# Sums of samples' halves and gate logits by a transposition and a VectorE sum in place of 0/1 products, and small gate and sample products merged or padded to 128 rows

## The chip, the cores and the metric

The kernel runs on one core of one Trainium2 chip. The metric is the time of one execution on the device in microseconds (us), the median of several runs. The names used here for the engines are those of the profile: PE is TensorE with its matrix products (PEld is the loading of its stationary operand), DVE is VectorE, ACT is ScalarE, POOL is GpSimd, and SP issues transfers.

## What is computed

The reference is one step of a hybrid decoder layer in float32: 1024 rows of a prompt and 32 rows of samples (8 sequences of 4 tokens) go through adaLN, one wide projection, an mLSTM branch with 4 heads, a sliding-window attention branch with 8 heads on 2 key/value heads, per-channel gates, and an output projection. Cut to what the change touches:

```
h, gate = adaln_in(x, c, w_ada, b_ada, g_norm)        # c: silu(c) @ w_ada, in three parts
(mq, mk, mv, mi, mf, mo, mz, aq, ak, av, az, gm, ga) = split_in(h @ w_in)
ig = mi + b_i                                         # the gate logits: 4 heads each
lf = log_sigmoid(mf + b_f)
b = cumsum(lf) per chunk of 128 rows                  # samples: per sequence of 4
...                                                   # mLSTM with exp(b - b + ig)
o = sink_attend(q, k, v)                              # samples: 128 cached rows and 4 own
u = sigmoid(gm) * (y_m @ w_mo) + sigmoid(ga) * (y_a @ w_ao)
x = x + gate * (u @ w_o)
```

## The kernel before, in words

PE is given its work in program order. The helper `mm` (line 275) issues one product and `tr` (line 280) one transposition, which is also a pass through PE; both advance a planning clock, `side.now`. A float32 product takes two passes on PE (`smpo` with 22 products has 44 rows in the profile), a transposition one. The large products, which make up most of the stream, are the projections of the prompt (`g_ak`, `g_av`, `g_aq`, `g_mq` ... and the pairs' `bx`, `by`, `bz`, `bw`); they use the full 128x128 array on pieces of 384, 288 or 512 columns. Between them stand small products of other work: attention units (`sc`, `pt`, `oT`), the mLSTM heads (`tk`, `tv`, `S`, `U`, `n`, `sU`, `sn`, `stk`), the samples, and the gates. Where these stand is set by `Side`, a planner: each kind of side work is a generator, which yields a lag and the PSUM banks that it needs next, and is resumed between large products when the planner's clock has passed the lag and the bank is free. PSUM has four tags of two banks each; the side work uses tags "b" (`pb`) and "o" (`po`). DVE and ACT carry out their instructions in the order of their queue, and a new tile in a bank waits until all readers of the tile before it in that bank are done.

The places that the change touches:

- **Gate logits.** `gate_piece` (line 596) multiplies the normalised rows with the gate columns in products of 32 columns each (`gg`), four partial sums in the four quarters of the partitions; ACT copies them to SBUF (`zg0`, `zg1`, `zg2`). `gate_sums` (line 607) then adds the four quarters: per block of 128 rows one product of `zg` with a 0/1 matrix of 8 columns into the PSUM tile `gp`; four blocks after the first piece, four after the second, one of 32 rows (the samples) after the third. `gates` (line 612) starts with that third call and goes on in DVE and ACT to `ig` and `lf`, then takes cumulative sums by products with triangular 0/1 matrices (`bp`, `gtp`), and later transposes a result (`fp`). Its pieces `bp`, `gtp`, `rp`, `bq`, `fp` and `fq2` stand between large products.
- **`kv_turn`** (line 797) transposes the values of the attention, first tile `vtp0`; it is started beside `gates`.
- **Samples' halves.** The projections of the 32 samples are not part of the large products: `Pair.samples` (16 products of a shape that uses 32 columns of the array, `smp`, or 8 for the output pairs, `smpa`) leaves four partial results in the four quarters of the partitions, that is two halves for each of two weight matrices; ACT copies them to `smps`. `samples_end` (lines 1392 and 1675) adds the halves with one product with a 0/1 matrix of 64 columns into the PSUM tile `smpo`, and the pair's own code reads that. There are 22 such calls: 4 pairs `head_in`, 8 `gate`, 2 `query_gate`, 4 `head_gate` and 4 output pairs.
- **Samples' attention** (line 915): `pts` are transpositions of the probabilities, `os` the products with the values, per half four with the cache (128 rows) and four with the samples' own values `vns` (32 rows).
- **`ada_gate`** (line 1943): twice `ada_products` (line 363), 8 products (4, a yield, 4) into one bank, `ada_ga`, 512 columns, on a quarter of the array's columns each.

Of the kernel before, what the change touches and what calls it, by code (L numbers as in the profile page):

```python
# [10 lines left out]
F32 = mybir.dt.float32  # L11
# [4 lines left out]
ALU = mybir.AluOpType  # L16
AX = mybir.AxisListType
# [18 lines left out]

C_ID, C_S9, C_TRI, C_CM, C_AM, C_TS, C_CS, C_RS, C_S32, C_BM, C_S64 = 0, 128, 137, 265, 393, 649, 681, 713, 745, 777, 785
C_END = 849
# [135 lines left out]
def body(tc, a):  # L174
    nc = tc.nc
    with ExitStack() as ctx:
# [429 lines left out]

        def gate_sums(gp, zg, cs):
            for c in cs:
                n = 128 if c < 8 else NS
                mm(gp[:n, c], zg[c // 4][:, c % 4 * 128:c % 4 * 128 + n], cst[:, C_S9:C_S9 + 8], start=True, stop=True)  # L610

        def gates(gp, zg, bias):
            gate_sums(gp, zg, (8,))
            ig = cp.tile([128, 36], F32, name="ig")
            gt2 = ht([128, 512], "gt2")
            x, e, r, q = (gt2[:, 256 + 36 * i:292 + 36 * i] for i in range(4))
            for t, o in ((ig, 0), (x, 4)):
# [6 lines left out]
            S.activation(e, e, AF.Exp, scale=-1.0)  # L624
            lf = sm([128, 36], "lf", 1)
            V.tensor_scalar(r, e, 2.0, None, op0=ALU.add)
# [12 lines left out]
            mm(bp[:, 0:36], tri, lf, start=True, stop=True)  # L639
            mm(bp[:NS, 64:68], cst[:NS, C_TS:C_TS + NS], lf[:NS, 32:36], start=True, stop=True)  # L640
            an = cp.tile([128, 36], F32, name="an")
            V.tensor_tensor(an, ig, bp[:, 0:36], op=ALU.subtract)
            V.tensor_tensor(an[:NS, 32:36], ig[:NS, 32:36], bp[:NS, 64:68], op=ALU.subtract)
            yield 4.0, "b"

            tp = pb([128, 4, 128], "gtp")
            tr(tp[:32, 0], an[:, 0:32], ident)
            mm(tp[:32, 1], lf[:, 0:32], tri, start=True, stop=True)
            tr(tp[:4, 2, 0:NS], an[:NS, 32:36], ident[:NS, :NS])
            mm(tp[:4, 3, 0:NS], lf[:NS, 32:36], cst[:NS, C_TS:C_TS + NS], start=True, stop=True)  # L650
            gt4 = ht([32, 4, 128], "gt4")
            aT, bT, zero, cm = (gt4[:, i] for i in range(4))
            nm, wi = gt2[:32, 0:128], gt2[:32, 128:256]
# [3 lines left out]
            V.tensor_copy(bT, tp[:32, 1])  # L657
            V.tensor_copy(aTs, tp[:4, 2, 0:NS])
            V.tensor_copy(bTs, tp[:4, 3, 0:NS])
            G.memset(zero, 0.0)  # L660
# [48 lines left out]
            fp = pb([128, 128], "fp")  # L709
            tr(fp[:, 0:32], bT, ident[:32, :32])  # L710
            fl = cp.tile([128, 32], F32, name="fl")
# [41 lines left out]
        def attention_begin():  # L753
            at["rope"] = [rope_load(p) for p in range(3)]
            at["vT"] = []
            at["sink"] = cp.tile([128, 2, 4], F32, name="sink")
            dma(at["sink"], a["sinks"].to_broadcast((128, 8)).rearrange("p (k g) -> p k g", g=4))
            at["qpad"] = cp.tile([128, NB, 2, 4, NT], F32, name="qpad")
            G.memset(at["qpad"], 0.0)
            at["kTs"] = cp.tile([128, NS], F32, name="kTs")  # L760
            at["vns"] = cp.tile([NS, 128], F32, name="vns")

# [34 lines left out]
        def kv_turn():  # L797
            kl, kTs, vT, kns, vns = at.pop("kl"), at["kTs"], at.pop("vT"), ht([128, 128], "kns")[:NS], at["vns"]
            for p, n in enumerate((3, 3, 2)):
                tp = pb([128, 3, 128], f"vtp{p}")  # L800
                for j in range(n):
                    tr(tp[:, j], vT[p][:, j * 128:(j + 1) * 128], ident)
                vn = ht([128, 3, 128], f"avn{p}")
                S.copy(vn[:, :n], tp[:, :n])
                dma(vnD[:, 3 * p:3 * p + n], vn[:, :n])
                if p < 2:
                    yield 4.0, "b"
            dma(a["v_p"], vn[:, 1])
            tp = pb([128, 3, 128], "kvtp")
            tr(tp[:, 0], kl[:, 128:256], ident)  # L810
            tr(tp[:NS, 1], kTs, ident)
            tr(tp[:NS, 2], vT[2][:, 256:288], ident)
            kn = ht([128, 128], "kl")
            V.tensor_copy(kn, tp[:, 0])
            V.tensor_copy(kns, tp[:NS, 1])
            V.tensor_copy(vns, tp[:NS, 2])
            dma(a["k_p"], kn)
            dma(a["k_s"][0:124], a["cache_k"][4:128])
            dma(a["v_s"][0:124], a["cache_v"][4:128])
            dma(a["k_s"][124:128].rearrange("t b e -> b t e"), kns)  # L820
            dma(a["v_s"][124:128].rearrange("t b e -> b t e"), vns)

# [92 lines left out]
        def sample_attention():  # L915
# [42 lines left out]
            for u in range(2):  # L958
                tr(pt[:, u], p[:, u, 0:WIN], ident)
                tr(pt[:NS, 2 + u], p[:, u, WIN:], ident)  # L960
            pT = kc[0]
            S.copy(pT[:, 0:2], pt[:, 0:2])
            V.tensor_copy(pT[:NS, 2:4], pt[:NS, 2:4])
            yield 7.0, "o"
            o = po([128, 2, 128], "os")
            for u in range(2):
# [3 lines left out]
                for w in range(4):  # L970
                    r = slice(32 * w, 32 * w + 32)
                    mm(o[r, u], pT[:NS, 2 + u, r], vns, start=False, stop=True, share=4)
            S.copy(p[:, :, 0:128], o)
# [394 lines left out]
        OPERANDS = {1: "b11", 2: "b21", 3: "b22", 4: "t4", 5: "t1", 6: "t2", 7: "t3"}  # L1368

        class Pair:  # L1370
            def __init__(self, kind, i):
# [20 lines left out]
            def samples_end(self):  # L1392
                o = pb([128, 64], "smpo")
                mm(o, self.sums, cst[:, C_S64:C_S64 + 64], start=True, stop=True)
                self.kind.samples(self, o.rearrange("p (c s) -> p c s", c=2))

# [249 lines left out]
        class AttPair:  # L1646
# [28 lines left out]
            def samples_end(self):  # L1675
                o = pb([128, 64], "smpo")
                mm(o, self.sums, cst[:, C_S64:C_S64 + 64], start=True, stop=True)
                us = ut[self.i % 2][:, self.i // 2 * 2:self.i // 2 * 2 + 2, SEQ:T]
                V.scalar_tensor_tensor(us, self.ts, 1.0, o.rearrange("p (c s) -> p c s", c=2), op0=ALU.add, op1=ALU.mult)

# [195 lines left out]
        for q, kk in enumerate(two):  # L1876
# [42 lines left out]
            if more:  # L1919
                x_mul(1, kept[1], two[q + 1])  # L1920
            else:
                pair_end(1, acc[1])
                gp = pb([128, 9, 8], "gp")
                gate_sums(gp, zg, range(4))
                gate_piece(wg, zg, 1)
            pair(kk, 2, acc[2])
        pair_end(2, acc[2])
        gate_sums(gp, zg, range(4, 8))
        gate_piece(wg, zg, 2)
# [13 lines left out]
        def ada_gate():  # L1943
            for j in range(2):
# [9 lines left out]
                acc = pb([128, 512], f"ada_ga{j}")  # L1954
                yield from ada_products(raws, acc)
                for r in range(0, 128, 32):
# [423 lines left out]
```

## Time and profile before

| | |
|---|---|
| time, median of 3 runs | 822.45 us (822.27 to 822.85) |
| the profiled execution's own time | 822.86 us |
| its span in the profile | 821.1 us |
| granted TensorE clock in it | 0.997 |
| busy PE, PEld, DVE, ACT, POOL | 98%, 81%, 73%, 51%, 6% of the span |

The profile is of one execution. A row of the timeline has the start in us from the span's start, the duration in us, the engine, the line, the operation, the tiles as out<-in (buffer numbers left out), the shapes and a count of instructions that ran on end; in square brackets stands the idle time ahead of it, if any, and what ended it. For PE the shape is rows\*columns of the array that the stationary operand takes, then the operand that streams through. Durations of PE's rows overlap, since passes are pipelined: what one costs is read from the starts of its neighbours.

### The profile page before, as it was taken

How to read it: one execution, taken by the hardware profiler on the slowest of the kernel's cores; microseconds unless marked ns; L12 is line 12 of the kernel's file. 1: busy time of each engine (PE TensorE's matmuls, PEld its weight loads, DVE VectorE, ACT ScalarE, POOL GpSimd, SP SyncE). 2: the span in 40 equal slices, each digit the busy share in tenths (PEclk: the TensorE clock that was granted, in tenths of full speed). 3: DMA queues.
4: the chain of work that ended last, by engine and by line, in shares of the span. 5: the costliest groups of instructions: out<-in, count | busy, mean ns of one | idle time of the engine just before them, and what ended most of it. 6: DMA issues, size and time to landing. Idle time of an engine off the chain costs nothing.

```text
span 821.1 us, 15097 instructions
## 1 busy us (share of the span) xinstructions
PE 803.2 (98%) x5145; PEld 666.1 (81%) x5145; DVE 598.6 (73%) x1495; ACT 419.2 (51%) x1020; POOL 46.5 (6%) x111
## 2 busy tenths in 40 slices
PE   6999999999999999999999999999999999999996
PEld 3779898888788878888888878788887789997775
DVE  4899886756755557475657889898668997876666
ACT  4764355556565564546555545554446652224334
POOL 0120000000000000000001011010002101000000
PEclk9999999999999999999999999999999999999998
DMA  9994757547545415537764685864436789647622
GB/s 338 395 330 136 228 167 221 166 155 208 173 138 171 148 60 162 163 131 254 238 213 152 229 265 186 266 216 141 142 100 193 237 294 393 211 140 284 205 104 109
DMA packets 113474, 165.49 MB, mean 202 GB/s; under 512 B 21185, under 2 KB 55745, under 8 KB 113365
## 3 DMA queue, kind: packets, MB, share of 16 engines
q1 hardware_dynamic: 107748, 153.78, 57.0%
q10 hardware_dynamic: 4176, 6.56, 2.2%
q0 software_dynamic: 1472, 4.20, 1.3%
q8 instruction: 40, 0.66, 0.3%
q14 instruction: 38, 0.30, 0.1%
HBM read 115.51 MB, written 50.00 MB: 202 GB/s over the span
## 4 chain that ended last, share of the span: by engine, by line
PE 88%; DVE 5%; DMA 3%; issue 2%; ACT 1%; SPq 0%; DVEq 0%; ACTq 0%
PE by L275 12%; PE bx L275 11%; PE bw L275 11%; PE g_w_mo L275 6%; PE bz L275 5%; PE g_aq L275 3%; PE foW L275 3%; PE foX L275 2%; PE foY L275 2%; PE smp L275 2%; PE g_mq L275 2%; PE sc L275 2%; PE oT L275 2%; PE n L275 2%; PE pt L280 2%
## 5 line engine op out<-in xcount | busy, mean ns | idle before, releaser
L220 ACT ACTIVATE p<-p,nmx 128x256 f32<-128x256 f32 (+1 forms) x64 | 31.1, 486 | 17.8 <-DVE nmx L220 15.2
L220 DVE CUSTOM_DVE_ANT_0 p<-sc,cst,sink 128x256 f32<-128x256 f32 (+1 forms) x64 | 26.1, 462 | 9.2 <-PE sc L275 9.1
L275 PE MATMUL g_aq<-h_h,wh_aq 128*128 128x384 f32 (+1 forms) x96 | 32.3, 336 | 0.0
L275 PE MATMUL g_aq<-h_h,wl_aq 128*128 128x384 f32 (+1 forms) x96 | 30.9, 322 | 0.0
L275 PE MATMUL g_aq<-h_l,wh_aq 128*128 128x384 f32 (+1 forms) x96 | 30.8, 321 | 0.0
L275 PE MATMUL g_w_mo<-ym_l,wh_w_mo 128*128 128x384 f32 (+1 forms) x96 | 30.8, 321 | 0.0
L275 PE MATMUL g_w_mo<-ym_h,wh_w_mo 128*128 128x384 f32 (+1 forms) x96 | 30.8, 321 | 0.0
L275 PE MATMUL g_w_mo<-ym_l,wl_w_mo 128*128 128x384 f32 (+1 forms) x96 | 30.8, 321 | 0.0
L220 DVE COPY p<-pt 128x512 f32<-128x512 f32 (+1 forms) x16 | 10.5, 656 | 16.9 <-PE pt L280 16.9
L220 ACT CAST wosh<-wor 128x512 fp32r<-128x512 f32 x24 | 14.8, 621 | 12.6 <-DVE wor L220 12.6
L275 PEld LDWEIGHTS g_aq<-h_h,wh_aq 128*128 128x128 f32 x96 | 18.0, 188 | 2.6 <-issue 1.5
L261 POOL DMA_DIRECT2D oD<-uqv x16 | 8.9, 557 | 182.9 <-ACT uqv L220 169.7
L220 DVE SCALAR_TENSOR_TENSOR tgw_mo<-tgw_mo,g_w_mo 128x384 f32<-128x384 f32 (+1 forms) x24 | 12.4, 518 | 8.7 <-PE g_w_mo L275 6.4
L220 DVE TENSOR_TENSOR wosl<-wor,wosh 128x512 fp32r<-128x512 f32 x24 | 16.5, 686 | 2.9 <-ACT wosh L220 2.7
L275 PE MATMUL sc<-ukv,uqv 64*128 64x256 f32 (+1 forms) x128 | 18.0, 390 | 0.4 <-DMA ukv<-kD 0.4
L275 PEld LDWEIGHTS g_w_mo<-ym_l,wh_w_mo 128*128 128x128 f32 x96 | 18.0, 188 | 0.0
L275 PEld LDWEIGHTS g_aq<-h_l,wh_aq 128*128 128x128 f32 x96 | 18.0, 188 | 0.0
L275 PEld LDWEIGHTS g_w_mo<-ym_h,wh_w_mo 128*128 128x128 f32 x96 | 18.0, 188 | 0.0
L275 PEld LDWEIGHTS g_w_mo<-ym_l,wl_w_mo 128*128 128x128 f32 x96 | 18.0, 188 | 0.0
L275 PEld LDWEIGHTS g_aq<-h_h,wl_aq 128*128 128x128 f32 x96 | 18.0, 188 | 0.0
L220 DVE TENSOR_TENSOR et<-et,S 128x384 f32<-128x384 f32 (+1 forms) x12 | 6.1, 510 | 15.8 <-PE S L275 15.8
L275 PE MATMUL g_mq<-h_h,wh_mq 128*128 128x384 f32 (+1 forms) x48 | 16.8, 350 | 0.3 <-ACT mk L220 0.3
(2063 smaller groups left out, 2806.8 us busy)
## 6 DMA issues: line engine op xcount, KB each, us to landing
x<-xT SPq DMA_DIRECT2D x16, 256.0 KB
early_h<-w_ada SPq DMA_DIRECT2D x8, 512.0 KB
adar_ga<-w_ada SPq DMA_DIRECT2D x16, 256.0 KB
wr_ga<-w SPq DMA_DIRECT2D x16, 256.0 KB
wr_gm<-w SPq DMA_DIRECT2D x16, 256.0 KB
taD<-gt SPq DMA_DIRECT2D x16, 256.0 KB
tmD<-gt SPq DMA_DIRECT2D x16, 256.0 KB
wor<-w_out SPq DMA_DIRECT2D x16, 256.0 KB
```

Of the source, the lines that this page charges most:

```text
L220: ins = f(*args, **kw)
L261: ins = (eng or nc.sync).dma_start(out, in_)
L275: in_order(nc.tensor.matmul(out, lhsT, rhs, start=start, stop=stop, skip_group_check=more))
L280: in_order(nc.tensor.transpose(out, in_, idn))
```

## The change

- `gate_sums` transposes each block of `zg` into a PSUM tile (`gp0`, `gp1`, `gp2`, one per piece, tag "b"), and one DVE sum over the four quarters per piece writes `gp`, which is now in SBUF.
- `samples_end` does the same with `smps` through the new `halves_sum`: one transposition into `smpo`, and a DVE sum that writes into `smps`; the pairs' code then reads SBUF instead of PSUM.
- The small products of the gates are merged or padded: `bp`'s second product takes 128 rows instead of 32; in `gtp` a transposition and a product of 160 columns stand for two transpositions and two products; `fp`'s transposition takes 128 rows instead of 32. The data that they need lie in 128 rows (`gt2`, `gt4`), parts of which POOL sets to zero, and DVE copies `an` once more. A constant moves beside another one.
- The samples' own values `vns` and their probabilities are padded with zeros to 128 rows, so all products of `os` have one shape; `pts` transposes 128 columns in place of 32.
- `ada_gate` passes over the yield between its two groups of four products.

```diff
-        def gate_sums(gp, zg, cs):
-            for c in cs:
-                n = 128 if c < 8 else NS
-                mm(gp[:n, c], zg[c // 4][:, c % 4 * 128:c % 4 * 128 + n], cst[:, C_S9:C_S9 + 8], start=True, stop=True)
+        def gate_sums(gp, zg, i):
+            n, m = (4, 128) if i < 2 else (1, NS)
+            tp = pb([128, 4, 128], f"gp{i}")
+            for c in range(n):
+                tr(tp[:m, c], zg[i][:, c * 128:c * 128 + m], ident)
+            V.tensor_reduce(gp[:m, 4 * i:4 * i + n], tp[:m, :n].rearrange("p c (g r) -> p c r g", r=32)[:, :, 0:8], op=ALU.add, axis=AX.X)
...
         def gates(gp, zg, bias):
-            gate_sums(gp, zg, (8,))
+            gate_sums(gp, zg, 2)
...
             gt2 = ht([128, 512], "gt2")
+            G.memset(gt2[:, 0:256], 0.0)
+            lf = gt2[:, 0:36]
...
             S.activation(e, e, AF.Exp, scale=-1.0)
-            lf = sm([128, 36], "lf", 1)
...
             mm(bp[:, 0:36], tri, lf, start=True, stop=True)
-            mm(bp[:NS, 64:68], cst[:NS, C_TS:C_TS + NS], lf[:NS, 32:36], start=True, stop=True)
+            mm(bp[:, 64:68], cst[:, C_TS:C_TS + 128], lf[:, 32:36], start=True, stop=True)
...
             V.tensor_tensor(an[:NS, 32:36], ig[:NS, 32:36], bp[:NS, 64:68], op=ALU.subtract)
+            V.tensor_copy(gt2[:, 128:164], an)
...
             tp = pb([128, 4, 128], "gtp")
-            tr(tp[:32, 0], an[:, 0:32], ident)
-            mm(tp[:32, 1], lf[:, 0:32], tri, start=True, stop=True)
-            tr(tp[:4, 2, 0:NS], an[:NS, 32:36], ident[:NS, :NS])
-            mm(tp[:4, 3, 0:NS], lf[:NS, 32:36], cst[:NS, C_TS:C_TS + NS], start=True, stop=True)
-            gt4 = ht([32, 4, 128], "gt4")
-            aT, bT, zero, cm = (gt4[:, i] for i in range(4))
+            tr(tp[:, 0], gt2[:, 128:256], ident)
+            sums = tp[:, 1:4].rearrange("p c e -> p (c e)")
+            mm(sums[:, 0:128 + NS], gt2[:, 0:128], cst[:, C_TRI:C_TRI + 128 + NS], start=True, stop=True)
+            gt4 = ht([128, 4, 128], "gt4")
+            G.memset(gt4[:, 1], 0.0)
+            aT, bT, zero, cm = (gt4[:32, i] for i in range(4))
...
             V.tensor_copy(bT, tp[:32, 1])
-            V.tensor_copy(aTs, tp[:4, 2, 0:NS])
-            V.tensor_copy(bTs, tp[:4, 3, 0:NS])
+            V.tensor_copy(aTs, tp[32:36, 0, 0:NS])
+            V.tensor_copy(bTs, sums[32:36, 128:128 + NS])
...
             fp = pb([128, 128], "fp")
-            tr(fp[:, 0:32], bT, ident[:32, :32])
+            tr(fp, gt4[:, 1], ident)
...
             at["kTs"] = cp.tile([128, NS], F32, name="kTs")
-            at["vns"] = cp.tile([NS, 128], F32, name="vns")
+            at["vns"] = cp.tile([128, 128], F32, name="vns")
+            G.memset(at["vns"], 0.0)
...
             V.tensor_copy(kns, tp[:NS, 1])
-            V.tensor_copy(vns, tp[:NS, 2])
+            V.tensor_copy(vns[:NS], tp[:NS, 2])
...
             dma(a["k_s"][124:128].rearrange("t b e -> b t e"), kns)
-            dma(a["v_s"][124:128].rearrange("t b e -> b t e"), vns)
+            dma(a["v_s"][124:128].rearrange("t b e -> b t e"), vns[:NS])
...
                 tr(pt[:, u], p[:, u, 0:WIN], ident)
-                tr(pt[:NS, 2 + u], p[:, u, WIN:], ident)
+                tr(pt[:, 2 + u], p[:, u, NS:], ident)
             pT = kc[0]
+            G.memset(pT[:, 2:4], 0.0)
             S.copy(pT[:, 0:2], pt[:, 0:2])
-            V.tensor_copy(pT[:NS, 2:4], pt[:NS, 2:4])
+            V.tensor_copy(pT[:NS, 2:4], pt[WIN - NS:, 2:4])
...
                     r = slice(32 * w, 32 * w + 32)
-                    mm(o[r, u], pT[:NS, 2 + u, r], vns, start=False, stop=True, share=4)
+                    mm(o[r, u], pT[:, 2 + u, r], vns, start=False, stop=True, share=4)
...
+        def halves_sum(sums):
+            o, t = pb([128, 2, 2, NS], "smpo"), sums[:, 0:2 * NS].rearrange("p (c s) -> p c s", c=2)
+            tr(o.rearrange("p c h s -> p (c h s)"), sums, ident)
+            V.tensor_reduce(t, o.rearrange("p c h s -> p c s h"), op=ALU.add, axis=AX.X)
+            return t
+
...
             def samples_end(self):
-                o = pb([128, 64], "smpo")
-                mm(o, self.sums, cst[:, C_S64:C_S64 + 64], start=True, stop=True)
-                self.kind.samples(self, o.rearrange("p (c s) -> p c s", c=2))
+                self.kind.samples(self, halves_sum(self.sums))
...
             def samples_end(self):
-                o = pb([128, 64], "smpo")
-                mm(o, self.sums, cst[:, C_S64:C_S64 + 64], start=True, stop=True)
                 us = ut[self.i % 2][:, self.i // 2 * 2:self.i // 2 * 2 + 2, SEQ:T]
-                V.scalar_tensor_tensor(us, self.ts, 1.0, o.rearrange("p (c s) -> p c s", c=2), op0=ALU.add, op1=ALU.mult)
+                V.scalar_tensor_tensor(us, self.ts, 1.0, halves_sum(self.sums), op0=ALU.add, op1=ALU.mult)
...
                 pair_end(1, acc[1])
-                gp = pb([128, 9, 8], "gp")
-                gate_sums(gp, zg, range(4))
+                gp = ht([128, 9, 8], "gp")
+                gate_sums(gp, zg, 0)
...
         pair_end(2, acc[2])
-        gate_sums(gp, zg, range(4, 8))
+        gate_sums(gp, zg, 1)
...
                 acc = pb([128, 512], f"ada_ga{j}")
-                yield from ada_products(raws, acc)
+                products = ada_products(raws, acc)
+                next(products)
+                yield from products
...
                 V.tensor_scalar(gb, gb, 0.25, None, op0=ALU.mult)
```

The planner's clock advances otherwise than before, so the order of the side work shifts against the large products. Three places of the program follow.

The first is PE where the third piece of the first projections ends. `gg` are the gates' partial products, `g_aq` the next projection, `vtp` the first transposition of `kv_turn`. Before:

```order
L275 MATMUL gp<-cst,zg_746 128x8 [waits Activation_49]
L275 MATMUL gp<-cst,zg_746 128x8 x3
L275 MATMUL gg_775<-small,wg 32x32 x8
L275 MATMUL g_aq_821<-h_h_378,wh_aq_0_691 128x384
L275 MATMUL g_aq_821<-h_l_379,wh_aq_0_691 128x384
L275 MATMUL g_aq_821<-h_h_378,wl_aq_0_692 128x384 [waits DVE_49]
L275 MATMUL gp<-cst,zg_784 32x8 [waits Activation_49]
L280 MATMUL vtp_854<-cst,vT_689 128x128 [waits PE_49]
L280 MATMUL vtp_854<-cst,vT_689 128x128 x2
```

And with the change:

```order
L280 MATMUL gp_774<-cst,zg_749 128x128 [waits DVE_49,Activation_49]
L280 MATMUL gp_774<-cst,zg_749 128x128 x3
L275 MATMUL gg_780<-small,wg 32x32 x8
L275 MATMUL g_aq_827<-h_h_378,wh_aq_0_692 128x384
L275 MATMUL g_aq_827<-h_l_379,wh_aq_0_692 128x384
L275 MATMUL g_aq_827<-h_h_378,wl_aq_0_693 128x384
L280 MATMUL gp_831<-cst,zg_789 32x128 [waits Activation_49]
L280 MATMUL vtp_861<-cst,vT_690 128x128 [waits DVE_49]
L280 MATMUL vtp_861<-cst,vT_690 128x128 x2
```

The products into `gp` have become transpositions into three tiles; the second of them, and `vtp`, now wait for DVE, where `vtp` waited for PE alone.

The second is DVE at the same place, from the last rotary embedding (`ropet`, `kr`, `krr`, `kTs`) to the first step of the gates. Before:

```order
L220 TENSOR_TENSOR ropet<-ropet,sin_556 128x288 [waits DMAHW2_49,DVE_49]
L220 TENSOR_TENSOR kr<-kr,cos_555 128x288
L220 TENSOR_TENSOR y_1_386<-y_1_386,x_5_94 128x512
L220 TENSOR_TENSOR krr<-kr,ropet 128x256 [waits DVE_49]
L220 TENSOR_TENSOR kTs<-kr,ropet 128x32
L220 TENSOR_TENSOR x_5_78<-x_5_78,y_1_386 128x512 [waits DMAHW7_49,DVE_49]
L220 TENSOR_TENSOR wl_aq_0_810<-wr_aq_0_805,wh_aq_0_809 128x512 [waits DMAHW7_49,PE_49,Activation_49]
L220 TENSOR_TENSOR wl_aq_1_814<-wr_aq_1_807,wh_aq_1_813 128x512 [waits DMAHW0_49,PE_49,Activation_49]
L220 TENSOR_TENSOR ig<-gp,gbias 128x32 [waits PE_49]
```

And with the change:

```order
L220 TENSOR_TENSOR ropet<-ropet,sin_556 128x288 [waits DMAHW2_49,DVE_49]
L220 TENSOR_TENSOR kr<-kr,cos_555 128x288
L220 TENSOR_TENSOR y_1_386<-y_1_386,x_5_94 128x512
L220 TENSOR_TENSOR krr<-kr,ropet 128x256 [waits DVE_49]
L220 TENSOR_TENSOR kTs<-kr,ropet 128x32
L220 TENSOR_REDUCE gp<-gp_774 128x32 [waits PE_49]
L220 MEMSET gt_835 128x36
L220 TENSOR_REDUCE gp<-gp_831 32x8 [waits PE_49]
```

The sum of `gp1` (tile number 774) stands behind the whole embedding; it is what `vtp` waits for on PE. The sum of `gp0` (734) stands further up, between the embedding of the piece before and three sums on `x`.

The third is PE in the first pair `query_gate`, in the changed kernel. `sU` are updates of an mLSTM head's sample states, which DVE adds to `Cs`; `bx` is a large product.

```order
L275 MATMUL bx<-h_l_578,wh_pquery_gate_2__6385 128x512
L275 MATMUL bx<-h_h_577,wl_pquery_gate_2__6386 128x512
L275 MATMUL sU_0_6476<-vm_6264,skn 128x388 [waits PE_49]
L275 MATMUL sU_1_6480<-vm_6269,skn 128x388
L275 MATMUL sU_2_6484<-vm_6274,skn 128x258
L275 MATMUL bx<-h_h_577,wh_pquery_gate_2__6385 128x512
L275 MATMUL bx<-h_l_578,wh_pquery_gate_2__6385 128x512
L275 MATMUL bx<-h_h_577,wl_pquery_gate_2__6386 128x512
L280 MATMUL smpo<-cst,smps 128x128 [waits DVE_49]
L275 MATMUL smp<-wr_az_0_6377,c_102 32x128 [waits DMAHW7_49,DVE_49]
```

Three products stand between `sU` and `smpo`, and both `smpo` and `smp` wait for DVE. In the kernel before, this call of `smpo` stood elsewhere against `sU`:

```order
L275 MATMUL bx<-h_h_576,wl_pquery_gate_2__6368 128x512
L275 MATMUL bx<-h_h_576,wh_pquery_gate_2__6367 128x512
L275 MATMUL bx<-h_l_577,wh_pquery_gate_2__6367 128x512
L275 MATMUL bx<-h_h_576,wl_pquery_gate_2__6368 128x512
L275 MATMUL smpo<-cst,smps 128x64 [waits PE_49]
L275 MATMUL smp<-wr_az_0_6359,c_102 32x128 [waits DMAHW2_49,DVE_49]
L275 MATMUL smp<-wr_az_1_6361,c_102 32x128 [waits DMAHW3_49]
```

There `smpo` waited for PE alone and came first; the three products of `sU` stand 43 rows of PE further on.

More of the change, by code (lines that the diff above doesn't have):

```diff
@@ L35 @@
 GROUPS = ((0, 1, 2), (3, 4, 5), (6, 7))
-C_ID, C_S9, C_TRI, C_CM, C_AM, C_TS, C_CS, C_RS, C_S32, C_BM, C_S64 = 0, 128, 137, 265, 393, 649, 681, 713, 745, 777, 785
+C_ID, C_S9, C_TRI, C_TS, C_CM, C_AM, C_CS, C_RS, C_S32, C_BM, C_S64 = 0, 128, 137, 265, 297, 425, 681, 713, 745, 777, 785
 C_END = 849
```

## The prediction

> **What bounds the kernel now.** The page comes first: the busy time of each engine, the granted clock, and the chain that ended last.
>
> ```profile
> span 821.1 us, 15097 instructions
> PE 803.2 (98%) x5145; PEld 666.1 (81%) x5145; DVE 598.6 (73%) x1495; ACT 419.2 (51%) x1020; POOL 46.5 (6%) x111
> PEclk9999999999999999999999999999999999999998
> PE 88%; DVE 5%; DMA 3%; issue 2%; ACT 1%; SPq 0%; DVEq 0%; ACTq 0%
> ```
>
> PE is busy for 98% of the span and makes 88% of the chain, at a granted clock of 9 tenths or more nearly throughout. Time taken out of its stream therefore reaches the end, unless PE waits for something in its place. The waits of PE (total, count, longest) show how little there is now between the start and the end:
>
> ```profile
> PE bx L275 <- DVE zt L220: 0.7, 1, 0.7
> PE sc L275 <- DMA ukv<-kD: 0.4, 1, 0.4
> PE g_mq L275 <- ACT mk L220: 0.3, 1, 0.3
> ```
>
> So two questions decide: what leaves PE's stream, and which new wait on DVE appears.
>
> **What leaves PE's stream.** Costs are read from starts, since durations overlap. First the 0/1 product of the halves, and a run of transpositions between large products:
>
> ```profile
> L275 PE MATMUL smpo<-cst,smps x44: 217/273/323, 220.4 to 678.8; 128*128 128x64 f32 x44
> 220.45 0.33 PE L275 MATMUL smpo<-cst,smps 128*128 128x64 f32 x2
> 220.70 0.30 PE L275 MATMUL smp<-wr_mq,c 128*32 128x128 f32 x2
> ...
> 221.72 0.50 PE L275 MATMUL bx<-h_h,wh_phead_in__2806 128*128 128x512 f32 x1
> 109.99 0.82 PE L280 MATMUL pt<-cst,p 128*128 128x128 f32 x6
> 110.56 0.42 PE L275 MATMUL g_aq<-h_h,wh_aq 128*128 128x384 f32 x1
> 110.82 0.33 PE L275 MATMUL g_aq<-h_l,wh_aq 128*128 128x384 f32 x1
> 110.99 0.34 PE L275 MATMUL g_aq<-h_h,wl_aq 128*128 128x384 f32 x1
> ```
>
> The two passes of `smpo` last 0.33 together and one 0.273, so the second starts 0.057 after the first; from there it takes 0.19 until the 32-column shape of `smp` starts (220.70). In a run, a transposition costs 0.57/6 = 0.095. The first large product behind small ones holds its successor up by 0.26 in place of 0.17, that is 0.09 for each interruption of the stream.
>
> *Halves, 22 times.* Two passes become one. I take the one pass step that goes, 0.057, as the wait before the other shape stays: 22 x 0.057 = 1.25. Bounds: from 0.25 to the run's 0.095, 3.4 in all; or from 0.25 to a transposition's whole duration of 0.272 (quoted under the rivals), a loss of 0.5.
>
> *Gate logits, and the gates' later pieces.*
>
> ```profile
> 58.37 0.95 PE L275 MATMUL gp<-cst,zg 128*128 128x8 f32 x8
> 59.25 0.62 PE L275 MATMUL gg<-y,wg 128*32 128x512 f32 x2
> 64.67 0.23 PE L275 MATMUL gp<-cst,zg 128*32 128x8 f32 x2
> 64.83 0.55 PE L280 MATMUL vtp<-cst,vT 128*128 128x128 f32 x3
> 84.35 0.27 PE L280 MATMUL gtp<-cst,an 128*32 128x128 f32 x1
> ...
> 85.15 0.44 PE L275 MATMUL g_aq<-h_h,wh_aq 128*128 128x384 f32 x1
> 130.26 0.34 PE L275 MATMUL g_mq<-h_h,wl_mq 128*128 128x384 f32 x1
> 130.53 0.24 PE L280 MATMUL fp<-cst,gt 32*128 32x32 f32 x1
> 130.71 0.44 PE L275 MATMUL g_mq<-h_h,wh_mq 128*128 128x384 f32 x1
> ```
>
> Eight passes into `gp` take 0.88; four transpositions take three steps of 0.095 and 0.19 before the other shape, 0.48. That is 0.40, twice. The third call takes 0.16 and becomes one pass: 0.10. Together **0.90**, all of it ahead of `vtp`. `gtp` takes 0.80 in three shapes; one transposition and two passes of 160 columns, at some 0.11 each, take 0.31: 0.49. `fp` takes 130.71 - 130.26 - 0.17 = 0.28 and becomes 0.095: 0.18. `bp` loses a shape too; I leave it at nothing (0 to 0.2).
>
> *Samples' attention and adaLN's gate.*
>
> ```profile
> 188.44 0.43 PE L275 MATMUL os<-vc,kc 128*32 128x128 f32 x8
> ...
> 189.86 0.55 PE L280 MATMUL pt<-cst,p 128*128 128x128 f32 x3
> 96.46 0.34 PE L275 MATMUL g_aq<-h_h,wl_aq 128*128 128x384 f32 x1
> 96.73 1.06 PE L275 MATMUL ada_ga<-adar_ga,c 128*32 128x512 f32 x8
> 97.73 0.45 PE L275 MATMUL g_aq<-h_h,wh_aq 128*128 128x384 f32 x1
> 43.00 0.29 PE L275 MATMUL g_av<-h_l,wh_av 128*128 128x288 f32 x1
> 43.22 1.93 PE L275 MATMUL ada_q<-adar_q,c 128*32 128x512 f32 x16
> 45.08 0.45 PE L275 MATMUL g_ak<-h_h,wh_ak 128*128 128x384 f32 x1
> ```
>
> The 32 passes of `os` take 1.42 in four stretches of alternating shape; 32 passes of `smp` in one shape take 221.72 - 220.70 = 1.02: 0.40 saved, though half of the passes now load 128 rows. An `ada_ga` half of 8 passes takes 97.73 - 96.46 - 0.17 = 1.10. `ada_q`, 16 passes in one go, takes 45.08 - 43.00 - 0.13 = 1.95. Two halves made one save 0.25 and one interruption, 0.09: 0.35, twice, 0.70.
>
> Sum for PE: 1.25 + 0.90 + 0.49 + 0.18 + 0.40 + 0.70 = **3.9 us**.
>
> **What is added elsewhere.** No row of this trace is a sum along an axis. The nearest is a copy of 128 columns out of PSUM, in the groups by line:
>
> ```profile
> L220 DVE COPY C<-U 128x129 f32<-128x129 f32 x4 | 1.2, 292 | 1.1 <-PE U L275 1.1
> 320.00:560.00 240.00, 239.34 (x1509) 198.65 (x1508) 181.45 (x423) 131.17 (x319) 17.31 (x60) 1.00 0.63 206
> ```
>
> I take 0.29 for each of the 25 sums, 7.3 us. DVE (the third busy time in the row by stretches) is busy for 181 of 240 us there and PE for 239, so PE's stream hides them; ACT's `gts` is delayed by one sum each. Without that cover a sum would cost its 0.29 and what is queued ahead of it. The zeroing on POOL (busy 6%) and the extra copy of `an` lie beside PE too; the gates' chain has products of `g_aq` all around it.
>
> **The new wait.** `vtp` takes the bank of `gp1` and must wait for DVE's sum of it. In DVE's queue that sum stands behind the whole rotary embedding:
>
> ```profile
> 61.19 1.29 DVE L220 TENSOR_TENSOR x<-x,y 128x512 f32<-128x512 f32 x2
> 62.41 0.68 DVE L220 TENSOR_TENSOR y<-y,x 128x512 f32<-128x512 f32 x1
> ...
> 63.30 0.48 DVE L220 STREAM_SHUFFLE ropet<-kr 128x288 f32<-128x288 f32 x1
> ...
> 65.94 0.18 DVE L220 TENSOR_TENSOR kTs<-kr,ropet 128x32 f32<-128x32 f32 x1
> 66.04 0.68 DVE L220 TENSOR_TENSOR x<-x,y 128x512 f32<-128x512 f32 x1
> ```
>
> DVE has no gap from 61.19 on but 62.41 + 0.68 to 63.30, some 0.2. The sum of `gp0` goes in ahead of 61.19 and pushes by 0.29, the gap takes 0.2 back. So the sum of `gp1` starts at 66.04 + 0.09 and ends at 66.42. PE comes to `vtp` at 64.83 - 0.90 = 63.93. It waits **2.5 us** (1.9 if DVE gets there 0.6 sooner, one of its 512-column steps; 2.9 if a sum along an axis lasts 0.68 like those), and all large products behind it wait too. This is where the gates' own gain goes, and more.
>
> What is late next: at 91 us PE waited 0.4 for a transfer of `ukv`. PE comes there 2.5 - 0.9 - 0.5 = 1.1 later than before, so that wait goes: -0.35.
>
> **Unknown.** In the second half the shifted order puts `smpo` three products behind `sU` in two `query_gate` pairs, waiting for DVE's additions into `Cs`, and a `smp` behind DVE's `gs` once. What is queued behind such a `smpo` is all of PE. These places don't exist in the trace. Below: 0, DVE being ahead. Above: three additions like `Cs` at 0.46, about 1.4 each, 4.1 in all:
>
> ```profile
> 529.39 1.36 DVE L220 TENSOR_TENSOR Cs<-Cs,sxb 128x387 f32<-128x387 f32 x3
> ```
>
> The nearest row is the only wait on DVE in that part, `bx` for `zt`, 0.7 once. I take 0.7 for the three together.
>
> Sum: -3.9 + 2.5 - 0.35 + 0.7 = -1.05. The profiled execution took 822.86 (span 821.1, 1.8 around it), so it would take 821.8; the median of the runs lies 0.4 lower: **821.4**.
>
> **The rivals.**
>
> (A) No stall at `vtp`: the sum is ready in time. For it: PE hardly waits for DVE anywhere. Against it: the queue order above. Without the stall, the 1.4 saved ahead of 91 us either pass on or run into the transfer of `ukv`, whose wait then grows. -3.9 + 0.7 = 819.2 to 820.6; I take 819.5. Chance 0.16.
>
> (B) The forecast, 821.4; its own range is 820.2 to 822.7. Chance 0.52.
>
> (C) Slower: in the `query_gate` pairs DVE's queue is behind, and each of the three waits costs its full 1.4. -3.9 + 2.5 - 0.35 + 4.1 = +2.4, 824.8. For it: DVE is at its fullest there and its queue in order. Against: between `sU` and `smpo` three products of 0.23 already hide half of one. It decides once the three cost 1.8 together, and is measurably slower from 3.4. Chance 0.18.
>
> (D) The change doesn't do what it says: a lone transposition is no cheaper than the two passes.
>
> ```profile
> L280 PE MATMUL pt<-cst,p x120: 270/272/329, 110.0 to 307.0; 128*128 128x128 f32 x120
> ```
>
> If `smp` starts only after the whole 0.272, the halves lose 0.5 in place of winning 1.25: 823.1. Against it: 0.095 each in a run. Chance 0.14.
>
> [...]
>
> **How the numbers follow.** A measurement of this kernel can tell 0.2%, 1.6 us, from no change: 820.8 is faster, 824.1 slower. (A) is faster whole; of (B) I put 0.18 below 820.8 and 0.34 within; of (C) 0.14 slower and 0.04 within; (D) within. Faster 0.34, same 0.52, slower 0.14. The range goes from (A) to near (C): 818.8 to 824.4.
>
> **What would show it.** In the waits of PE, `vtp` on DVE's `gp` with about 2.5; the `ukv` wait gone. `smpo` to `smp` in 0.19 (0.27 would be (D)). `os` in one stretch of about 1.0, `ada_ga` in two of 1.95. Waits of `smpo` or `smp` on `Cs` or `gs` would show (C). PE's busy time falls by 3 to 5 us. The forecast is wrong if the shuffled order opens a wait at a place not named here, or DVE reaches the sum of `gp1` before 64 us.

## The result, and the profile after

| | before | with the change |
|---|---|---|
| median, us (6 runs each) | 823.04 (822.27 to 825.2) | 828.09 (827.39 to 829.63) |
| ratio, 95% interval | | 1.0061 (1.0046 to 1.0075) |
| profiled execution, its span | 822.86, 821.1 | 828.02, 826.2 |

The change makes the kernel 5.0 us slower, where 1.0 us faster was forecast, and the time lies above the range. The page shows the first half of the puzzle: PE's busy time hardly moved, its share fell, and so the loss is time in which PE stood still or ran slowly.

```profile
span 826.2 us, 15068 instructions
PE 802.8 (97%) x5111; PEld 663.1 (80%) x5111; DVE 606.9 (73%) x1521; ACT 420.4 (51%) x1020; POOL 45.4 (5%) x115
```

Before, PE had four short waits behind the start: the three that the prediction shows (0.7, 0.4 and 0.3), and one of an attention unit's transposition near 198 us:

```profile
PE pt L280 <- DVE mx L220: 0.5, 1, 0.5
```

With the change the waits of 0.3 and more are these (total, count, longest):

```profile
PE vtp L280 <- DVE gp L220: 2.0, 1, 2.0
PE oT L275 <- DVE mx L220: 1.0, 1, 1.0
PE g_aq L275 <- ACT aq L220: 1.0, 1, 1.0
PE smpo L280 <- DVE Cs L220: 0.9, 2, 0.5
PE sc L275 <- DMA ukv<-kD: 0.8, 1, 0.8
PE aw L275 <- ACT aw L220: 0.5, 1, 0.5
PE bw L275 <- ACT bw L220: 0.4, 1, 0.4
PE g_ak L275 <- DVE h_h L220: 0.3, 1, 0.3
```

The first is the forecast one. The timeline of PE shows what followed it:

```profile
63.96 0.27 PE L280 MATMUL gp<-cst,zg 128*32 128x128 f32 x1
66.27 0.55 PE L280 MATMUL vtp<-cst,vT 128*128 128x128 f32 x3 [2.04 <-DVE gp L220]
66.57 0.42 PE L275 MATMUL g_aq<-h_h,wh_aq 128*128 128x384 f32 x1
66.83 0.33 PE L275 MATMUL g_aq<-h_l,wh_aq 128*128 128x384 f32 x1
67.00 0.34 PE L275 MATMUL g_aq<-h_h,wl_aq 128*128 128x384 f32 x1
67.18 0.41 PE L275 MATMUL g_aq<-h_h,wh_aq 128*128 128x384 f32 x1
67.39 0.52 PE L275 MATMUL g_aq<-h_l,wh_aq 128*128 128x384 f32 x1
67.70 0.52 PE L275 MATMUL g_aq<-h_h,wl_aq 128*128 128x384 f32 x1
```

And the busy times by stretches of 1 us, whose third value from the end is the granted clock (1.00 is full speed):

```profile
66.00:67.00 1.00, 0.73 (x6) 0.73 (x6) 1.00 (x7) 0.15 (x1) 0.00 (x0) 1.00 0.00 0
67.00:68.00 1.00, 1.00 (x5) 0.98 (x5) 1.00 (x7) 0.97 (x3) 0.00 (x0) 0.66 0.00 0
68.00:69.00 1.00, 1.00 (x5) 1.00 (x5) 1.00 (x3) 0.99 (x2) 0.00 (x0) 0.50 0.63 215
69.00:70.00 1.00, 1.00 (x5) 1.00 (x4) 1.00 (x4) 0.12 (x1) 0.00 (x0) 0.50 0.80 176
70.00:71.00 1.00, 1.00 (x5) 1.00 (x4) 1.00 (x3) 0.00 (x0) 0.00 (x0) 0.63 0.98 350
71.00:72.00 1.00, 1.00 (x7) 1.00 (x7) 0.42 (x2) 0.00 (x0) 0.00 (x0) 1.00 0.77 223
```

PE stood idle for 2.0 us. A microsecond after it started again the granted clock fell to one half, and the steps of `g_aq`, from start to start, went from 0.17 to 0.32; at 70.7 it was back. The missing clock, 0.34 + 0.50 + 0.50 + 0.37 in the four rows, is 1.7 us on top of the wait. Not every execution pays this: of the six, four have a mean granted clock of 0.994 or 0.995 (828.02 to 829.63 us), two one of 0.998, as high as in the kernel before (827.39 and 827.74 us).

A ledger places the rest. All large products stand in the same order in both kernels, so the n-th of them can be compared, though small products that stood ahead of it in one kernel can stand behind it in the other, which moves single rows by 1 us or more:

| large product | starts before | after | later by |
|---|---|---|---|
| 101st, `g_ak` | 50.77 | 50.64 | -0.1 |
| 201st, `g_aq` | 74.42 | 77.45 | 3.0 |
| 301st, `g_aq` | 94.56 | 99.28 | 4.7 |
| 401st, `g_aq` | 115.76 | 121.51 | 5.8 |
| 1301st, `bw` | 391.37 | 395.18 | 3.8 |
| 1901st, `by` | 560.30 | 566.26 | 6.0 |
| 2501st, `g_w_mo` | 700.12 | 705.27 | 5.2 |

The stall at `vtp` costs 3 us; a second loss falls between 77 and 100 us, a third near 110; then some 2 us are won back, though a wait at 198 us lies there too; and between 395 and 566 us another 2 us go. Of the 2 us won back only half is the savings in the stream: between the same two products e11 below, which has these savings and not the merge, gains 1.0, and e5, the merge alone, gains 0.9, since small products have moved. The second loss, on PE:

```profile
95.02 0.93 PE L275 MATMUL sc<-ukv,uqv 64*128 64x128 f32 x8 [0.83 <-DMA ukv<-kD]
95.88 2.85 PE L275 MATMUL ada_ga<-adar_ga,c 128*32 128x512 f32 x16
98.65 0.44 PE L275 MATMUL g_aq<-h_h,wh_aq 128*128 128x384 f32 x1
```

The 16 merged passes of `ada_ga` take 2.85 where 16 passes of `ada_q` took 1.93. SP issues weights for `ada_ga` as late as from 93.1 on:

```profile
93.09 1.38 SPq L261 DMA_DIRECT2D adar_ga<-w_ada  x3
```

The last loss, at the first `query_gate` pair, on DVE:

```profile
530.81 0.69 DVE L220 TENSOR_TENSOR ws<-wr_az,wr_az 128x512 f32<-128x512 f32 x1 [1.21 <-DMA wr_az<-w]
531.42 1.35 DVE L220 TENSOR_TENSOR Cs<-Cs,sU 128x387 f32<-128x387 f32 x3
```

In the new order a sum on weights stands ahead of the additions into `Cs` and waits for its transfer; `smpo` on PE waits for `Cs`, from 531.62 to 532.02, and `smp` behind it again.

### The profile page after: what moved, and what is told of

It is laid out like the page before. It is cut to its first block, busy times and chain, and to the rows that moved or that the text cites. A ratio compares the mean times of both kernels' runs of the same rounds, so it can differ in the third digit from the quotient of the medians.

```text
span 826.2 us, 15068 instructions
## 1 busy us (share of the span) xinstructions
PE 802.8 (97%) x5111; PEld 663.1 (80%) x5111; DVE 606.9 (73%) x1521; ACT 420.4 (51%) x1020; POOL 45.4 (5%) x115
## 5 line engine op out<-in xcount | busy, mean ns | idle before, releaser
L220 ACT ACTIVATE p<-p,den 128x256 f32<-128x256 f32 (+1 forms) x32 | 14.4, 490 | 6.3 <-DVE den L220 6.3
L220 ACT COPY uqv<-oT 128x256 f32<-128x256 f32 x16 | 5.9, 368 | 21.4 <-PE oT L275 21.2
```

The lines of the kernel that those rows point to most:

```text
L220: ins = f(*args, **kw)
```

## The experiments

Two theories stood: (1) the loss is the stall at `vtp` with the half clock, plus waits from the shifted order of the side work, while the savings in the stream are real; (2) the savings are not there, or the sums on DVE eat them. The first expectations call them theory 1 and theory 2. The first four kernels are timed beside 823.06 (822.01 to 824.06) for the kernel before.

**e1_sum_early**: one statement moved in the changed kernel, so that DVE's sum of `gp1` stands ahead of the rotary embedding.

```diff
+        gate_sums(gp, zg, 1)
         pair_end(2, acc[2])
-        gate_sums(gp, zg, 1)
```

> The changed kernel with one statement moved: the sums of the second piece of gate logits stand ahead of pair_end(2), so that on VectorE the sum of gp1 comes ahead of the last rotary embedding. Theory 1 (the loss comes from two things: the wait of vtp for that sum with the halved TensorE clock behind it, and new waits elsewhere from the shifted order of the side work): the wait of 2.0 us falls below 0.3, the granted clock stays at 1.0 between 66 and 72 us, which gives 1.6 more, so 3.7 us come off and 824.4 is reached, unless the transfer of ukv near 94 us doesn't come earlier and its wait of 0.8 grows by what was won. Theory 2 (the stall at vtp is hidden by that transfer anyway): the wait for ukv grows to about 4 us, and the time stays at 827 to 828.

826.21 us, ratio 1.0042 (1.0025 to 1.0059). The wait of `vtp` and the half clock are gone, but 1.9 us come off, not 3.7: PE now comes earlier to the place at 89 us, where it waits 1.0 for ACT, and waits 0.9 for `ukv` at 92. Both theories were half right.

**e2_gates_only**: the kernel before with the gate logits' edit; each transposition advances the planner's clock by what the product did before.

```diff
-        def tr(out, in_, idn):
-            side.now += 0.11
+        def tr(out, in_, idn, cost=0.11):
+            side.now += cost
```

> The kernel before with the gate logits' part alone (transpositions into gp0 to gp2, three sums on VectorE, gp in SBUF); the planner's clock advances as before, so the order of the side work is that of before. Theory 1: vtp waits for about 2.0 us and the clock is halved for about 3.4 us behind it (1.6 lost), against 0.9 saved: 2.7 slower than before, less the 0.4 of the ukv wait, 825.2 beside 823.0. Theory 2: the transfer of ukv sets the time at 92 us in both, and it is within 0.5 of before.

825.43, ratio 1.0024 (1.0012 to 1.0036): `vtp` waits 2.0, and the clock is at 0.57 from 66 to 70 us. The edit alone costs 2.4 us.

**e3_halves_only**: the kernel before with `halves_sum`, planner's clock kept.

> The kernel before with the samples' halves alone (transposition and VectorE sum in samples_end), planner's clock and order of before. Theory 1 (what was saved in the stream is real, and the waits of smpo on Cs come from the shifted order): smpo with its 16 smp costs 1.21 in place of 1.27, no wait of smpo on Cs, 1.2 us faster than before, 821.8 beside 823.0. Rival (the sums on VectorE delay others, the waits come from them): no faster than before, with waits of PE on VectorE at the query_gate pairs.

822.35, ratio 0.999 (0.9981 to 1.0). No wait on `Cs` appears. `smpo` with its 16 products `smp` takes 1.21 in place of 1.27, which in 22 calls is some 1.2 us out of the stream; 0.5 of it comes back in a wait of `aw` for ACT at 645 us, where PE is now early. This run also waited 1.0 for `ukv` at 92 us, ahead of the edit's first use, in place of 0.4: that transfer's arrival varies between runs.

**e4_all_in_old_order**: all parts but the merge of `ada_ga`, sum of `gp1` early, planner's clock kept; PE's order is that of before.

> All parts of the change but the merged halves of ada_ga, with the planner's clock advanced as before, so that PE's order is that of before but for gtp's two rows fewer, and with the sum of gp1 ahead of the rotary embedding. Theory 1: no new waits, 3.9 less 0.7 for ada_ga comes off, 819.8 beside 823.0. Rival (the savings in the stream are not there, or come back as waits whatever the order): 822.5 or more.

821.88, ratio 0.9988 (0.9979 to 0.9998). That is 4.3 us below e1, which has the merge and the order that comes with it. Of the 3.2 expected, 1.2 are reached. The three largest waits of PE that are new or have grown:

```profile
PE g_aq L275 <- ACT aq L220: 1.2, 1, 1.2
PE sc L275 <- DMA ukv<-kD: 0.9, 1, 0.9
PE aw L275 <- ACT aw L220: 0.5, 1, 0.5
```

ACT's queue shows behind what the first of these stands:

```profile
88.83 0.62 ACT L220 CAST wh_aq<-wr_aq 128x512 fp32r<-128x512 f32 x1 [7.32 <-DMA wr_aq<-w]
89.36 0.48 ACT L220 ACTIVATE aq<-g_aq 128x384 f32<-128x384 f32 x1
```

The cast waits for weights, and the copy of `g_aq` that PE needs is queued behind it. The weights come at 88.8 here and at 89.3 in e10, though PE is further on here. The stretches between large products (the time from one to the next, less its own step, where small products stand between) add up to 147.5 us in this profile and to 150.2 in that of before, while the idle gaps in them grew from 1.0 to 1.5: some 3.2 us were taken out, as worked out.

Which edit shifts the order? Without the merge but with its own planner's clock, the changed kernel has the old order on PE; the kernel before with the merge alone has the new one, at every place but `gtp`. The next four, beside 823.13 (822.65 to 823.96):

**e5_ada_only**: the merge alone, on the kernel before.

```diff
-                yield from ada_products(raws, acc)
+                products = ada_products(raws, acc)
+                next(products)
+                yield from products
```

> The kernel before with the merged halves of ada_ga alone (the yield between the two groups of four products is passed over). Built, its order on PE is that of the changed kernel at every place but gtp: the merge alone shifts the side work. Theory 1 (the merge costs more by the shifted order than it saves): 0.7 saved, and the waits of the changed kernel at 110 us (g_aq for ACT, 1.0), 198 us (oT for the maximum, 1.2, in place of the 0.5 of pt before), 455 us (0.4) are there without any other part; the waits of smpo on Cs near 530 and 555 us (0.5 each) as well: 2 to 3 us slower than before, 825 to 826. Rival (those waits need the sums on VectorE or the padded products): 0.7 faster, 822.4.

829.2 (827.23 to 830.44), ratio 1.0074 (1.0055 to 1.0092). The merge alone is as slow as the whole change, and its mean clock is that of the kernel before (0.997 or 0.998 in all four runs), so this loss needs no half clock. Apart from `vtp`, its longest waits are those of the changed kernel, and one for weights:

```profile
PE smpo L275 <- DVE Cs L220: 1.6, 2, 1.1
PE oT L275 <- DVE mx L220: 1.0, 1, 1.0
PE g_aq L275 <- ACT aq L220: 1.0, 1, 1.0
PE ada_ga L275 <- DMA adar_ga<-w_ada: 0.9, 1, 0.9
```

`smpo` here is still the 0/1 product: that wait has nothing to do with transpositions or sums. The wait for weights is larger than it looks: from the start of the first `ada_ga` to the next product it takes 4.1 us, where the second one, which waits for nothing, takes 1.85.

**e6_ada_kept_order** and **e8_all_kept_order**: the merge, with the planner shown two groups at the old places; on the kernel before, and on e4.

```diff
-                yield from ada_products(raws, acc)
+                products, now = ada_products(raws, acc), side.now
+                next(products)
+                half = side.now - now
+                now = side.now
+                next(products)
+                side.now = now
+                yield 2.0, "b"
+                side.now += half
+                side.products += 1
+                yield 2.0, ""
```

> The kernel before with the merged halves of ada_ga, but the planner is shown them as two groups: the clock and the yields are as before, so all other side work keeps its place. Theory 1: 0.7 faster than before and no new wait: 822.4 beside 823.1. Rival (eight products in one go hold up the large products and their evacuation by themselves): 823 or more.

> All parts of the change, the sum of gp1 ahead of the rotary embedding, the planner's clock as before, and the merged ada_ga shown to the planner as two groups, so that all side work keeps the place it had before. Theory 1: 0.7 below the kernel e4_all_in_old_order, 821.2 beside 823.1 for before; the waits at 89 and 92 us stay or grow by 0.35, since one merged group stands ahead of them or right behind. Rival (what is saved goes into waits whatever is done): 821.9 or more.

827.88, ratio 1.0055 (1.004 to 1.0071), and 826.98, 1.0053 (1.0036 to 1.007). Theory 1 falls here: keeping PE's order doesn't save the merge. Both show one wait that neither order had, and e6's timeline of ACT shows how it arises:

```profile
120.77 0.62 ACT L220 CAST wh_mk<-wr_mk 128x512 fp32r<-128x512 f32 x1 [1.75 <-PE g_aq L275]
...
124.61 0.57 ACT L220 COPY p<-pt 128x512 f32<-128x512 f32 x1
125.09 0.47 ACT L220 ACTIVATE aq<-g_aq 128x384 f32<-128x384 f32 x1
```

```profile
125.61 0.69 PE L275 MATMUL g_mq<-h_h,wh_mq 128*128 128x384 f32 x1 [2.29 <-ACT aq L220]
```

The cast of the next weights stands in ACT's queue ahead of an attention unit's work and waits 1.75 for PE. Before, that place in the queue held no such cast, and `aq` came over 3 us sooner:

```profile
121.74 0.47 ACT L220 ACTIVATE aq<-g_aq 128x384 f32<-128x384 f32 x1
```

With `aq` late, PE waits 2.3, and the clock halves from 125 to 132 us. The half clock is not the whole of it: two of e6's four runs have a mean clock of 0.998 and still take 825.62 and 828.08.

**e7_filled_wait**: the changed kernel with ten products of constants ahead of `vtp`; their result is not used.

> The changed kernel with ten extra products of two constant 128x128 tiles on PE between gp2 and vtp; their result is not used. They take about 2.0 us of the wait of 2.04. Theory 1 (TensorE's clock is halved because PE idles for 2 us): the wait goes down to near 0, the granted clock stays at 1.0 between 66 and 72 us, and the 1.6 us of the half clock come off, unless the waits at 89 to 95 us take them up: 826.4 to 828.1, with the vtp transpositions at the same place, near 66.3. Rival (the drop has another cause, as the transpositions or VectorE's load): the clock drops all the same.

827.18, from 824.14 to 830.23, ratio 1.0048 (1.0034 to 1.0061). The clock stays at 1.0 between 50 and 418 us: with the idle time filled, no half clock came behind `vtp`. The profiled run, the slowest of the nine, shows the same effect at another place: DVE waited 2.6 for `wr_az` in place of 1.2, `smpo` waited 1.8 on `Cs`, and the clock halved there: the steps of `by` are 0.43 in place of 0.23.

```profile
532.25 0.33 PE L280 MATMUL smpo<-cst,smps 128*128 128x128 f32 x1 [1.82 <-DVE Cs L220]
533.73 0.69 PE L275 MATMUL by<-t3h,wh_pquery_gate__6443 128*128 128x512 f32 x1
534.21 0.63 PE L275 MATMUL by<-t3l,wh_pquery_gate__6443 128*128 128x512 f32 x1
534.64 0.63 PE L275 MATMUL by<-t3h,wl_pquery_gate__6444 128*128 128x512 f32 x1
```

The last four are timed beside 823.24 (822.5 to 825.44).

**e9_late_merge**: e4 with the merge, the eight products at the place of the second group, so that their weights have come.

```diff
+                side.now += 4 * 512 / 2400
+                side.products += 1
+                yield 2.0, "b"
+                now = side.now
+                for _ in ada_products(raws, acc):
+                    pass
+                side.now = now + 4 * 512 / 2400
+                yield 2.0, ""
-                yield from ada_products(raws, acc)
```

> As e4_all_in_old_order, with the eight products of each ada_ga merged at the place of the second group, not of the first, the planner being shown two groups: all other side work keeps its place, and the weights of the second group have as long to arrive as before. Theory (the merge costs by reading its second group's weights and freeing buffers earlier, and by the shifted order, not by being one run of eight): 0.7 below e4, that is 821.2 beside 823.1 for before, and no wait of ada_ga for adar_ga. Rival (eight in one go hold up the stream's evacuation wherever they stand): a new wait of g_aq, g_mq or g_mk for ACT, 822 or more.

826.57 (823.82 to 828.76), ratio 1.0037 (1.0023 to 1.0052): a miss. `ada_ga` no longer waits for weights, but `g_mk` waits for ACT for 1.7 in the profiled run. That run is the fastest, 2.0 above the profiled run of e4, and its clock holds; the mean clock of the five others is 0.992 to 0.996, as low as in the profiled runs with a half clock (0.993 to 0.996), but none of the five has a trace. ACT's queue again, here and in e4:

```profile
140.97 0.62 ACT L220 CAST t3h<-x 128x512 fp32r<-128x512 f32 x1 [1.94 <-DMA qD<-mk]
...
143.37 0.48 ACT L220 ACTIVATE mk<-g_mq 128x384 f32<-128x384 f32 x1
```

```profile
138.82 0.62 ACT L220 CAST t3h<-x 128x512 fp32r<-128x512 f32 x1 [0.68 <-PE ada_ga L275]
...
139.85 0.47 ACT L220 ACTIVATE mk<-g_mq 128x384 f32<-128x384 f32 x1
```

In e4 the cast `t3h` takes a buffer that a group of `ada_ga` has just given back; with the group later, it takes one whose store is still under way, and the evacuation of `g_mq` stands behind it. The 16 weight tiles of `ada_ga` come from the pool of 50 shared buffers, so the merge moves not only products but the times at which buffers come free.

**e10_no_early_parts**: the kernel before with the halves and the padded `os`, `pts`, `vns` and `fp` only.

> The kernel before with the halves, the padded os, pts and vns and the padded fp, without the gate logits, bp, gtp and ada_ga; order of before. Theory (what is saved ahead of 92 us runs into transfers that arrive when they do, wr_aq at 89 and ukv at 92 us): the same time as e4_all_in_old_order, 821.9, though 1.4 us less is taken out of PE's stream; the waits at 89 and 92 us are shorter by as much. Rival (the early savings count): 823.1 or more, 1.2 above e4.

821.49, ratio 0.998 (0.9972 to 0.9989), the fastest kernel here. It saves 1.75, where 1.8 were worked out for its parts (1.25, 0.18 and 0.40). e4, which takes 1.4 more out of the stream ahead of 92 us, is no faster: it waits 1.2 at 89 us and 0.9 for `ukv`, and e10 only 1.0 for `ukv`.

**e11_no_merge**: the changed kernel without the merge.

> The changed kernel without the merged halves of ada_ga, and with the sum of gp1 where the change has it. Its order on PE is that of before. Theory (vtp's stall and the merge are two separate losses that add): e4's 821.9 plus the stall, of which e1 got back 1.9: 823.8 to 824.3, none of the waits at 110, 198, 455, 530 and 555 us. Rival (the losses overlap): 826 or more, or below 822.5.

823.75, ratio 1.0 (0.9991 to 1.0008). The stall at `vtp` and the merge add up: 1.9 above e4, and 4.3 below the change. The half clock shows again (0.69 from 66 to 70 us and 0.88 from 70 to 74 in the profile): nine of its runs have a mean clock of 0.995 (822.87 to 824.73 us), two have 0.997 and 0.998 (822.37 and 821.64).

**e12_gates_filled**: e2 with five filling products ahead of `vtp`; result unused.

> The kernel e2_gates_only with five extra products of two constant 128x128 tiles on PE between gp2 and vtp, their result unused; about 1.0 us of work inside the wait of 2.0, so PE idles for 1.0. Theory (the clock is halved after an idle of 1.8 us or more, and not after one of 1.2 or less, as in all kernels so far): the clock stays at 1.0 between 66 and 72 us, vtp starts where it did, and 1.6 us come off: 823.8 beside 825.4 for e2, unless the ukv wait takes part of it. Rival (the drop comes with the wait for VectorE itself): the clock drops again, 825.4.

823.75, ratio 1.0005 (0.9996 to 1.0013), 1.7 below e2. PE idles 0.9 and the clock holds:

```profile
63.89 1.28 PE L275 MATMUL fill<-one 128*128 128x128 f32 x10
66.08 0.55 PE L280 MATMUL vtp<-cst,vT 128*128 128x128 f32 x3 [0.92 <-DVE gt L220]
```

## Why the prediction was wrong

5.0 us slower was measured, 1.0 faster was forecast. Two steps of the sum failed above all: the merge of `ada_ga`, put at 0.70 saved, costs 4 to 6 us; and the wait of `vtp`, put at its length, costs up to 1.7 more through the half clock. The prediction's own sign of being wrong came with it, a wait at a place not named.

- **What leaves PE's stream** was right: 3.9 were worked out, and e4, without the 0.7 of the merge, shows 3.2. The terms, in the profile after: `gp` 0.35 twice (0.40 given), `gtp` 0.52 (0.49), `fp` 0.24 (0.18), `os` 1.01 in place of 1.42 (0.41; 0.40 given), `smpo` to `smp` 0.20, 0.055 less a call (0.057). Rival (D), no gain from a lone transposition, is refuted by the last.
- **The wait of `vtp`** was right as a wait: from start to start 2.2 for the 2.5 given (2.0 from the modelled end of the pass before), as the sum ended 0.2 sooner and PE came 0.1 later. So the stall that rival (A) left out did come. It was wrong as a price. The step took a wait to cost what it lasts; the half clock behind it cost 1.7 more in the profiled run (e12 got back 1.7 in the median with the idle time halved).
- **"That wait goes: -0.35"** was wrong. PE came to `ukv` 2.5 later and still waited 0.8. The place was read as a fixed arrival; but SP issued the transfer 2.9 later (the rows below), and its arrival varies besides. And what is saved ahead of 92 us was let pass to the end, where e10 reaches e4's time without it: `wr_aq` and `ukv` came no sooner when PE did. This was told under rival (A) and not put into the sum.
- **The merge of `ada_ga`** is the step that failed most. It was put at 0.70 saved, from the structure of the passes. That saving exists where nothing waits: the second `ada_ga` takes 1.85 in the change's profile, in place of 1.00 twice. In all it costs: e5, the merge alone, is 6 us slower than before, and e11, the change without it, 4.3 faster than the change. Three things were left out: its second group reads weights that land only then (0.9 at 96 us); it alone shifts the planner's order at all places but one; and it changes when the 16 buffers come free (e9) and where ACT's casts stand (e6, e8). The prediction laid the shuffled order to the change as a whole, and priced it at 0.7 for three places; it opened waits at 110, 198 and 455 us that were not named.
- **Rival (C)** named the right place and mechanism for part of it: `smpo` on `Cs`, twice, 0.8 each with what `smp` waits behind it, where 0.7 for all three was taken and up to 1.4 each was the bound. At the first of the two it wasn't the sums on DVE that were late, but a step on weights that waited for its transfer ahead of `Cs`; at the second, at 555 us, the additions stand behind four steps on weights in a queue without a gap.

The issue of `ukv` on SP, before and with the change:

```profile
89.73 0.42 SPq L261 DMA_DIRECT2D ukv<-kD  x1
```

```profile
92.62 0.42 SPq L261 DMA_DIRECT2D ukv<-kD  x1
```

With the sizes of the profile the sum nearly closes: 3.9 saved; given back 2.2 + 1.7 at `vtp`, 0.5 more at `ukv` and 0.9 for the weights of `ada_ga`, 1.0 at 110 us, 1.2 less the 0.5 of before at 198, 0.4 at 455, 1.6 less the 0.7 of `zt` at the `query_gate` pairs, 0.5 for `aw`, 0.3 for `h_h` at 53 us; less the 0.3 of `mk`: +4.9, and the spans differ by 5.1. Single terms are less sure than the total: from the 101st to the last large product the change falls 3.8 behind e11, where the merge's terms here come to 2.9.

What stays open: how the merge's 4 to 6 us divide between late weights, shifted order and buffers. Four ways to merge gave three sets of waits, and none that lost nothing; that the buffers are the cause in e9 is read from who released the cast, why the cast of e6 stands further ahead in ACT's queue isn't shown, and no run changes the buffers alone.

## What to carry to other kernels

Where PE is the bound and its stream is planned, the edit to fear is not the one that adds instructions but the one that passes over a yield or gives buffers back at another time: rebuild with that edit alone and compare the order before pricing it. A wait on an in-order engine is priced by what stands behind it in the queue: in e4 a cast on ACT that waited for weights cost PE 1.2 through the copy behind it. An idle of PE of 1.8 to 2.3 us was followed in this kernel's profiles by a half clock, which took 1.7 us more at `vtp` and some 3.4 in e6 (the missing clock by stretches). Time saved ahead of a transfer that came no sooner was worth nothing (e4, 821.88, takes 1.4 more out there than e10, 821.49), while savings behind it counted in full (e10: 1.75 of 1.8).

## What the runs showed of the hardware

- The granted clock fell to one half after idles of PE that the prediction priced at their length alone. Behind the start, gaps of 1.8 (e7), 2.0 (the change, e2, e11) and 2.3 us (e6, e8) were each followed by a stretch at 0.5; gaps of 1.7 and 1.4 (e9), 1.2 (e4) and 0.9 (e12) were not. The clock that is missing behind the gap adds up to 1.7 us in the change, e2, e8 and e11, and to 3.4 in e6; in e7 the steps of `by` went from 0.23 to 0.43. Ahead of the gap stand transpositions in the change (`gp`) and large products in e7 (`bx`).
- Whether every such idle is followed by a half clock is not shown: two of the change's six runs have a mean clock of 0.998, and two of e11's eleven 0.997 and 0.998, where the profiled ones have 0.995; none of the four has a trace. No run shows what else decides it.
- A wait of passes for a transfer did not show as a gap in the change's profile: the 16 of `ada_ga` took 2.85 in place of 1.93 there. Two of them started when weights landed, at 96.8 and 97.6 us, while rows of other passes, 0.6 long, still covered the time. e5's profile names the transfer with 0.9, where the passes take 2.3 us longer (4.1 in place of 1.85), and e7's with 0.6.
